# The gate of the S5 branch cut into token chunks, and the first scores' tiles in a pool of their own

## The chip, the cores and the metric

One core of one Trainium2 chip runs the whole step. The metric is device time in microseconds, here the median of three runs; a profile of one execution, with its own time, stands beside it. The core's engines have one instruction stream each: PE (matmuls), ACT (activations), DVE (vector), POOL (a second, slower vector engine), and SP, which here only issues DMA transfers. Each stream is worked off in order, so an instruction that waits holds up all that stand behind it on its engine.

## The reference

One layer over T = 1056 tokens (1024 of a prompt, 32 of a decode step): RMSNorm, one input projection, two branches (attention with 8 heads of 64, and an S5 state-space model), an output projection, a final norm. The part that the change touches is the S5 branch behind its scan:

```
y = gelu(y)
y = y * sigmoid(y @ w_glu + b_glu)                 # the gated linear unit
ssm_o = rmsnorm(y, g_ssm) * silu(gs)               # gs: a slice of the input projection
```

The first attention scores follow in time. They are `z = q @ k.T / 8`, and the weights are built from `sigmoid(z)` and a running product of `sigmoid(-z)` along the keys ("stick breaking", no softmax).

## The kernel before

Tokens are worked in three chunks, `TC = [(0, 256), (256, 384), (640, 416)]`. Channels lie on the 128 partitions, four groups `m` of them, so the S5 output is `y_nat` [128, 4, 1056] in the on-chip memory.

The kernel's order of work is fixed when the program is built. Projections (`proj`) are generators that emit matmuls; beside them run tasks, which are resumed after each step of a projection. A task yields a name (it goes on when that piece of work has been emitted), a number of steps, or a time of a clock kept by rough costs (`at`, `dve`). That clock decides only where in the streams an instruction is put. `put` issues a store one step later on SP's queue.

The stretch in question begins when the scan's last output is in (`open_glu`). Then PE interleaves the matmuls of the gated linear unit (`glu(0)`, `glu(1)`, `glu(2)`, one per chunk, four groups of twelve matmuls `z<-yh`, `z<-yl` each) with the projections q0, k0 and v0 (`pj<-xh,w_hi` and the like), in three chunks each. Each `glu(i)` splits its chunk into a high and a low half (`yh` by ACT, `yl` by DVE); after each group ACT forms the sigmoid `sg`, DVE multiplies it into `y_nat`, ACT squares, and POOL adds the squares up in `sqS`, from which the norm's sum comes.

`ssm_gate` follows `glu2`. For each of the four channel groups it loads `gs` [128, 1056] from DRAM, DVE multiplies `y_nat` by `gssm` and `gs` (one scalar_tensor_tensor), ACT forms `sgs = sigmoid(gs)`, POOL multiplies that in, and the group is stored to `ssm_d`, where it is read much later. Two `gs` tiles exist, in the place of `yl` and `yh`. At the end `sums` turns the squares into one number per token on PE (nine matmuls by a column of ones), and `rsqrt` makes the inverse root `rsS` by six small operations on POOL, on 9 columns (one per 128 tokens).

Then the pool of `y_nat` and of the other temporaries is closed, and the tiles of the attention are laid out in the memory that comes free: `qB1`, `kB1`, `kL1`, `vS1` first, then the two buffers `cb` for the running products, the mask row `own`, and the `betaS` and `betaL` tiles. POOL clears half of `kL1` and most of `own` on the way. The first unit of the attention (`s1_unit`) emits score matmuls `z<-kA,qA`; ACT writes `sigmoid(-z)` into `cb` and `sigmoid(z)` into `betaL`; DVE scans `cb` (with `own`), and POOL multiplies the result into `betaL`, which PE transposes later. PE has two banks for `z`, so it can run at most two score tiles ahead of ACT. The projections that follow are woven in between as filler.

Of the kernel before, what the change touches and what calls it, by code (L numbers as in the profile page):

```python
# [8 lines left out]
F32 = mybir.dt.float32  # L9
F32R = mybir.dt.float32r  # L10
BF = mybir.dt.bfloat16
I32 = mybir.dt.int32
AF = mybir.ActivationFunctionType
# [12 lines left out]
NB = 134  # L26
NK = 25
RSS = 28
LEAD = 1
WARM = 9  # L30
WL = {1: ((1, slice(0, 1)),), 2: ((0, slice(1, 3)), (1, slice(1, 3))), 4: ((0, slice(3, 8)),), 5: ((1, slice(3, 8)),)}
# [188 lines left out]
def hymba_step(ctx, tc, xT, xn, w_in, ln_g, kcT, vc, w_glu, b_glu, w_out, g_att, g_ssm, final_g,  # L220
# [26 lines left out]
    def act(out, in_, f=AF.Copy, **kw):  # L247
        nc.scalar.activation(out, in_, f, **kw)

    def tt(out, a, b, op, eng=None):  # L250
        (eng or nc.vector).tensor_tensor(out, a, b, op)
# [76 lines left out]
    def rsqrt(out, src, inv_n, t1, t2):  # L328
        g = nc.gpsimd
        ts(t1, src, inv_n, EPS, OP.mult, OP.add, g)  # L330
        tt(out, t1, mhalf[:t1.shape[0]].to_broadcast(list(t1.shape)), OP.pow, g)
        tt(t2, out, out, OP.mult, g)
        tt(t2, t2, t1, OP.mult, g)
        ts(t2, t2, -0.5, 1.5, OP.mult, OP.add, g)
        tt(out, out, t2, OP.mult, g)

    def sums(rs, sq):
        pp = p_tr()
        s_, a_, b_ = rsc, rst[:, 0], rst[:, 1]
        nc.vector.memset(s_, 1.0)  # L340
        for b in range(9):
            n = min(128, T - 128 * b)
            nc.tensor.matmul(pp[:n, b:b + 1], sq[:, 128 * b:128 * b + n], ones,
                             start=True, stop=True)
        nc.vector.tensor_copy(s_[:, 0:8], pp[:, 0:8])
        nc.vector.tensor_copy(s_[0:TS, 8:9], pp[0:TS, 8:9])
        rsqrt(rs, s_, 1.0 / 512, a_, b_)

    s2 = ExitStack()
    ss = s2.enter_context(tc.tile_pool(name="ss", bufs=1))  # L350
# [26 lines left out]
    def x_sq(b):  # L377

        m, _ = blk(b)
        nc.scalar.activation(xq[b][:m], xq[b][:m], AF.Square, accum_out=rst[:m, 1, b:b + 1])  # L380

    xq = {}
    rsc = const.tile([128, 9], F32, name="rsc")
# [194 lines left out]
    def at(*aps, lead=0.0):  # L578

        return lambda: nc.ready(*aps) - lead  # L580
# [74 lines left out]
    def put(dst, src):  # L655

        later.append([PUT, lambda: nc.sync.dma_start(dst, src)])
# [85 lines left out]
    with ExitStack() as s1:  # L743
# [449 lines left out]
        def open_glu():  # L1193
            yield "y3"
            yield "GW"
            nc.sync.dma_start(st_out, fin)
            s2.close()
            open_pair0()
            gl = s1.enter_context(tc.tile_pool(name="gl", bufs=1, side="right"))
            G["p"] = gl  # L1200
            Y1["sq"] = gl.tile([128, T], F32, name="sqS")
            done.add("G")

        def lag(m):
# [12 lines left out]
        def glu_y(i):  # L1217
            t0, n = TC[i]
            gl = G["p"]
            yh = gl.tile([128, 4, NM], F32R, name="yh")  # L1220
            yl = gl.tile([128, 4, NM], F32R, name="yl")
            act(yh[:, :, :n], Y1["y"][:, :, t0:t0 + n])
            tt(yl[:, :, :n], Y1["y"][:, :, t0:t0 + n], yh[:, :, :n], OP.subtract)
            YH[i] = yh, yl

        def glu(i):

            yield "G" if i == 0 else f"glu{i - 1}"
            glu_y(i)
            t0, n = TC[i]  # L1230
            yh, yl = YH[i]
            yield at(yh[:, :, :n], yl[:, :, :n], G["h"], G["l"])
            for m in range(4):
                ps = p_z()
                for k in range(4):
                    for f, (a, b) in enumerate(((G["h"], yh), (G["h"], yl), (G["l"], yh))):
                        nc.tensor.matmul(ps[:, :n], a[:, k, m * 128:(m + 1) * 128], b[:, k, :n],
                                         start=(k == 0 and f == 0), stop=(k == 3 and f == 2))
                sg = G["p"].tile([128, NM], F32, name="sg", bufs=2)
                act(sg[:, :n], ps[:, :n], AF.Sigmoid, bias=bglu[:, m:m + 1])  # L1240
                yv = Y1["y"][:, m, t0:t0 + n]
                tt(yv, yv, sg[:, :n], OP.mult)
                sq = Y1["sq"][:, t0:t0 + n]
                if m == 0:
                    act(sq, yv, AF.Square)
                else:
                    act(sg[:, :n], yv, AF.Square)
                    tt(sq, sq, sg[:, :n], OP.add, nc.gpsimd)
                yield 2
            done.add(f"glu{i}")  # L1250

        tg = {}

        def gate_load(m):
            tg[m] = G["p"].tile([128, T], F32, name="gs", tag=("yl", "yh")[m % 2])
            nc.sync.dma_start(tg[m], gs_d[:, m])

        def ssm_gate():
            yield "glu2"
            gate_load(0)  # L1260
            gate_load(1)
            for m in range(4):
                yield at(tg[m], lead=500.0)
                yv = Y1["y"][:, m]
                nc.vector.scalar_tensor_tensor(yv, yv, gssm[:, m:m + 1], tg[m], OP.mult, OP.mult)
                sg = Y1["p"].tile([128, T], F32, name="sgs", tag="bst", bufs=2)
                act(sg, tg[m], AF.Sigmoid)
                tt(yv, yv, sg, OP.mult, gp)
                put(ssm_d[:, m], yv)
                if m < 2:  # L1270
                    gate_load(m + 2)
                yield dve(yv)
            yield at(Y1["sq"])
            sums(rsS, Y1["sq"])

        at_step(2, 20, spawn, glu_weights())
        at_step(6, 0, spawn, open_glu())
        for i in range(3):
            at_step(6, 0, spawn, glu(i))
        at_step(6, 0, spawn, ssm_gate())  # L1280

        def until(f):
            while f not in done:
# [26 lines left out]
    p1 = ctx.enter_context(tc.tile_pool(name="p1", bufs=1))  # L1310
    Q["sqA"] = p1.tile([128, T], F32, name="sqA")
    s3 = ctx.enter_context(ExitStack())
    at = s3.enter_context(tc.tile_pool(name="at", bufs=1))
    qB[1] = at.tile([128, TP], F32R, name="qB1")
    kB[1] = at.tile([128, TP], F32R, name="kB1")
    kL[1] = at.tile([128, TP], F32R, name="kL1")
    nc.gpsimd.memset(kL[1][0:64].bitcast(F32), 0.0)
    vS[1] = at.tile([128, 8, 128], F32, name="vS1")
    NC_ = 2
    cbuf = [at.tile([128, CW], F32, name=f"cb{i}") for i in range(NC_)]  # L1320

    own = at.tile([128, TP], BF, name="own")
    nc.gpsimd.memset(own[:, 0:TP - 128], 0.0)
    nc.vector.tensor_copy(own[:, TP - 128:TP], ident)
    n_c = [0]
# [14 lines left out]
    def beta(n):  # L1340

        if n <= 512:
            return at.tile([128, 512], F32, name="betaS", bufs=2)
        return at.tile([128, CW - 1], F32, name="betaL", bufs=4)

    def c_tile():
        n_c[0] += 1
# [242 lines left out]
    def pipeline():  # L1590

        units = []
        for p in range(4):
            for h in range(2):
                for j in (3, 0, 2, 1):
                    units.append((p, h, j))
                    if (p, h, j) in DEC:
                        units.append(("dec", DEC.index((p, h, j))))
        live = []

        def tail(u, out):
            if u[0] == "dec":
                yield from decode_s3(u[1], out[0])
            else:
                yield from s3_unit(*u, *out)

        for i, u in enumerate(units + [None, None]):
            out = []
            if u is None:
                first = iter(())  # L1610
                n1 = 0
            elif u[0] == "dec":
                first = decode_s1(u[1], out)
                n1 = 6
            else:
                p, h, j = u
                if (h, j) == (0, 3):
                    yield f"qkv{p}"
                ratio[0] = RATIO[2 * p + h]
                first = s1_unit(p, h, j, out)  # L1620
                n1 = 2 * (1 + j // 2)
            second, n3 = iter(()), 0
            if len(live) == 2 or u is None:
                v = live.pop(0)
                second = tail(*v)
                n3 = 13 if v[0][0] == "dec" else 2 * v[0][2] + 2

            if units[i + 1:i + 2] and units[i + 1] and units[i + 1][0] == "dec":
                for n in range(4):
                    k_load(units[i + 1][1], n)  # L1630
            a = b = 0
            e1 = e3 = False
            yield 0.0
            while not (e1 and e3):
                if not e1 and (e3 or a * n3 <= b * n1):
                    a += 1
                    x = next(first, None)
                    e1 = x is None
                else:
                    b += 1  # L1640
                    x = next(second, None)
                    e3 = x is None
                if x is not None:
                    yield x
            if u is not None:
                live.append((u, out))
                if u[0] != "dec" and u[1:] == (0, 1):
                    flags.add(f"A{u[0]}")
                if u[0] != "dec" and u[1:] == (1, 1):
                    flags.add(f"S1_{u[0]}")  # L1650
        while pvq:
            yield pop_pv()
# [415 lines left out]
```

## Time and profile before

| | us |
|---|---|
| median of 3 runs (lowest to highest) | 681.17 (680.73 to 681.33) |
| the profiled execution | 682.8 |
| its span, first to last instruction | 680.9 |
| PE busy in the span | 626.7 (92%) |
| DVE, ACT, POOL busy | 429.1, 346.3, 228.1 |
| mean granted TensorE clock | 0.968 of full |

The profiled execution took 1.9 us more than its span, and 1.6 us more than the median of the runs. PE is the busiest engine by far, so what counts is where it stands still, or runs at the lower of its two clock levels. The page's line of PE and its line of the granted clock show those places, in 40 slices of 17 us each.

### The profile page before, as it was taken

What the parts mean: (1) busy time and instruction counts of PE and PEld (TensorE: products, weight loads), DVE (VectorE), ACT (ScalarE), POOL (GpSimd) and SP (SyncE); (2) the same over time, 40 slices, a digit from 0 to 9 for tenths busy, and PEclk for the clock granted to TensorE, in tenths of its full rate; (3) what the DMA queues carried; (4) which work ended last, traced back from release to release, by engine and by line L of the source; (5) the groups of instructions that cost most, each with busy time, mean ns of one, the idle gap of its engine ahead of it and who ended that gap; (6) DMA issues with size and microseconds to landing.
All of it is one profiled execution on the core that took longest, in us unless ns stands there. A gap on an engine that the chain in (4) does not pass through costs nothing.

```text
span 680.9 us, 10474 instructions
## 1 busy us (share of the span) xinstructions
PE 626.7 (92%) x3760; PEld 523.9 (77%) x3760; DVE 429.1 (63%) x670; ACT 346.3 (51%) x787; POOL 228.1 (33%) x334
## 2 busy tenths in 40 slices
PE   7948999999969993899999999999998899997995
PEld 6938899988969993788878698886775566756873
DVE  5947999889335443465776565656557948364654
ACT  5572423252555643566766657555765645442332
POOL 0011122000122167444345343432417513133885
PEclk7969999999979996999999999999999999998999
DMA  8726342552520144210221112333162795218552
GB/s 307 270 90 175 95 143 79 178 167 66 177 69 24 56 166 153 67 36 25 64 87 59 46 44 74 95 103 102 39 184 92 254 286 178 69 63 269 182 172 100
DMA packets 64132, 83.46 MB, mean 123 GB/s; under 512 B 9040, under 2 KB 47248, under 8 KB 64080
## 3 DMA queue, kind: packets, MB, share of 16 engines
q1 hardware_dynamic: 57600, 71.23, 32.4%
q10 hardware_dynamic: 6480, 11.56, 5.4%
q8 instruction: 30, 0.49, 0.3%
q14 instruction: 22, 0.18, 0.1%
HBM read 56.29 MB, written 26.48 MB: 122 GB/s over the span
## 4 chain that ended last, share of the span: by engine, by line
PE 69%; POOL 6%; DMA 5%; ACT 4%; issue 3%; DVE 3%; SPq 1%; DVEq 0%; POOLq 0%; ACTq 0%
PE pj L215 36%; PE z L215 14%; PE pv L215 10%; PE tr L215 8%; POOL rst L215 2%; DMA gs<-gs_d 1%; DMA x<-in_xn 1%; POOL rsA L215 1%; DMA w_raw<-in_w_in 1%; DMA yj<-yd 1%; DVE cb L215 1%; DMA yd<-Y 1%; SPq L215 1%; POOL s__6538 L215 0%; DMA O<-att_d 0%
## 5 line engine op out<-in xcount | busy, mean ns | idle before, releaser
L215 PE MATMUL pj<-xh,w_hi 128*128 128x256 f32 (+2 forms) x472 | 163.9, 350 | 0.0
L215 PE MATMUL pj<-xl,w_hi 128*128 128x256 f32 (+2 forms) x472 | 151.4, 324 | 0.0
L215 PE MATMUL pj<-xh,w_lo 128*128 128x256 f32 (+2 forms) x472 | 151.3, 323 | 0.0
L215 PEld LDWEIGHTS pj<-xh,w_hi 128*128 128x128 f32 x472 | 89.9, 190 | 23.7 <-issue 19.8
L215 DVE TENSOR_TENSOR_SCAN cb<-cb,own 128x896 f32<-128x896 f32 (+3 forms) x64 | 96.5, 1514 | 15.0 <-ACT cb L215 12.8
L215 PEld LDWEIGHTS pj<-xl,w_hi 128*128 128x128 f32 x472 | 90.2, 191 | 1.7
L215 PEld LDWEIGHTS pj<-xh,w_lo 128*128 128x128 f32 x472 | 89.5, 190 | 0.3
L215 ACT ACTIVATE cb<-z 128x512 f32<-128x512 f32 (+4 forms) x102 | 49.8, 488 | 53.0 <-PE z L215 34.7
L215 PE MATMUL pj<-xh,S 128*128 128x512 f32 (+3 forms) x212 | 69.4, 405 | 2.1 <-DVE x L215 1.5
L215 POOL TENSOR_TENSOR betaL<-betaL,cb 128x896 f32<-128x896 f32 (+2 forms) x24 | 41.4, 1725 | 60.8 <-DVE cb L215 36.9
L215 POOL TENSOR_TENSOR w_lo<-w_raw,w_hi 128x512 fp32r<-128x512 f32 x30 | 46.5, 1550 | 44.3 <-ACT w_hi L215 44.3
L215 ACT ACTIVATE wt<-tr 128x512 f32<-128x512 f32 (+2 forms) x86 | 47.2, 552 | 16.6 <-PE tr L215 16.3
L215 PE MATMUL pv<-wt,vS 128*64 128x256 f32 x320 | 52.0, 404 | 1.1 <-POOL wt L215 1.1
L215 POOL TENSOR_TENSOR betaS<-betaS,cb 128x128 f32<-128x128 f32 (+3 forms) x32 | 27.1, 851 | 73.2 <-DVE cb L215 38.3
L215 PEld LDWEIGHTS pj<-xh,S 128*128 128x128 f32 (+2 forms) x212 | 36.2, 184 | 17.2 <-issue 7.5
L215 DVE TENSOR_TENSOR kv_out<-pj,rsx 128x256 f32<-128x256 f32 (+2 forms) x55 | 28.3, 514 | 29.5 <-PE pj L215 29.0
L215 PE MATMUL pj<-xl,S 128*128 128x512 f32 (+3 forms) x112 | 43.1, 387 | 0.0
L215 ACT ACTIVATE w_hi<-w_raw 128x512 fp32r<-128x512 f32 x44 | 27.6, 630 | 27.0 <-DMA w_raw<-in_w_in 17.0
L215 PE MATMUL tr<-ident,betaL 128*128 128x128 f32 x226 | 35.8, 276 | 4.1 <-ACT wt L215 2.6
L215 ACT ACTIVATE betaL<-z 128x512 f32<-128x512 f32 (+4 forms) x70 | 35.8, 512 | 0.0
L215 PEld LDWEIGHTS tr<-ident,betaL 128*128 128x128 f32 x226 | 26.9, 141 | 11.1 <-ACT wt L215 3.4
L215 DVE TENSOR_TENSOR attT<-pv,attT 64x256 f32<-64x256 f32 x32 | 13.4, 420 | 32.6 <-ACT attT L215 32.4
(273 smaller groups left out, 1273.3 us busy)
## 6 DMA issues: line engine op xcount, KB each, us to landing
w_raw<-in_w_in ACTq DMA_DIRECT2D x44, 256.0 KB, 2.6
xq<-in_xn SPq DMA_DIRECT2D x8, 512.0 KB, 7.4
x<-in_xn SPq DMA_DIRECT2D x8, 512.0 KB, 5.7
yp_d<-x SPq DMA_DIRECT2D x8, 512.0 KB, 2.9
x<-yp_d SPq DMA_DIRECT2D x8, 512.0 KB, 5.2
y_out<-x SPq DMA_DIRECT2D x8, 512.0 KB, 2.9
xr<-in_xT SPq DMA_DIRECT2D x7, 528.0 KB, 8.6
wraw<-in_w_out SPq DMA_DIRECT2D x5, 512.0 KB, 5.3
```

Of the source, the lines that this page charges most:

```text
L215: return g(*args, **kw)
```

## The change

The gate is done chunk by chunk. `gate(i)` is a task that starts when `glu(i)` and `gate(i - 1)` have been emitted, and `glu(2)` now also waits for `gate(0)`. A gate loads its chunk of `gs` in two halves of two channel groups each, into two tiles of their own; per half there are one sigmoid (ACT), two scalar_tensor_tensor (DVE), one product over both groups and one store. The products of chunks 0 and 1 are POOL's, those of chunk 2 DVE's (`GPG`). The squares' tile is per chunk, and `sums` is called per chunk: chunk 0 has 2 columns, chunk 1 has 3, chunk 2 has 4. The root follows at once for chunks 0 and 1. For chunk 2 only the sums are copied out; its root, and the clearing of `kL1`, are issued behind the attention's second unit. The tiles `cb`, `own` and `beta` come from a pool `az`, opened ahead of the pool with `qB1`, `kB1`, `kL1` and `vS1`.

```
+GPG = (1, 1, 0)
-    def sums(rs, sq):
+    def sums(i, rs, sq):
...
+        if i < 2:
+            rsqrt(rs[:, c], s_, 1.0 / 512, a_, b_)
...
+            if i == 2:
+                yield "gate0"
             glu_y(i)
...
+            Y1["sq", i] = G["p"].tile([128, NM], F32, name="sqS", bufs=2)
...
-        def ssm_gate():
-            yield "glu2"
-            gate_load(0)
-            gate_load(1)
-            for m in range(4):
-                yield at(tg[m], lead=500.0)
-                yv = Y1["y"][:, m]
-                nc.vector.scalar_tensor_tensor(yv, yv, gssm[:, m:m + 1], tg[m], OP.mult, OP.mult)
-                sg = Y1["p"].tile([128, T], F32, name="sgs", tag="bst", bufs=2)
-                act(sg, tg[m], AF.Sigmoid)
-                tt(yv, yv, sg, OP.mult, gp)
-                put(ssm_d[:, m], yv)
-                if m < 2:
-                    gate_load(m + 2)
+        def gate(i):
+
+            yield f"glu{i}"
+            if i:
+                yield f"gate{i - 1}"
+            t0, n = TC[i]
+            cs = slice(t0, t0 + n)
+            g = [G["p"].tile([128, 2, NM], F32, name="gs", bufs=2) for _ in range(2)]
+            for h in range(2):
+                nc.sync.dma_start(g[h][:, :, :n], gs_d[:, 2 * h:2 * h + 2, cs])
+            for h in range(2):
+                gh = g[h][:, :, :n]
+                yield at(gh, lead=300.0)
+                sg = Y1["p"].tile([128, 2, NM], F32, name="sgs", tag="bst", bufs=2)
+                act(sg[:, :, :n], gh, AF.Sigmoid)
+                for m in (2 * h, 2 * h + 1):
+                    yv = Y1["y"][:, m, cs]
+                    nc.vector.scalar_tensor_tensor(yv, yv, gssm[:, m:m + 1], gh[:, m % 2], OP.mult, OP.mult)
+                yv = Y1["y"][:, 2 * h:2 * h + 2, cs]
+                tt(yv, yv, sg[:, :, :n], OP.mult, GPG[i] and gp)
+                put(ssm_d[:, 2 * h:2 * h + 2, cs], yv)
                 yield dve(yv)
-            yield at(Y1["sq"])
-            sums(rsS, Y1["sq"])
+            sums(i, rsS, Y1["sq", i])
+            done.add(f"gate{i}")
...
+    az = s3.enter_context(tc.tile_pool(name="az", bufs=1))
+    cbuf = [az.tile([128, CW], F32, name=f"cb{i}") for i in range(2)]
+    own = az.tile([128, TP], BF, name="own")
     at = s3.enter_context(tc.tile_pool(name="at", bufs=1))
...
-    nc.gpsimd.memset(kL[1][0:64].bitcast(F32), 0.0)
...
+            if i == 1:
+                nc.gpsimd.memset(kL[1][0:64].bitcast(F32), 0.0)
+                rsqrt(rsS[:, 5:9], rsc[:, 5:9], 1.0 / 512, rst[:, 0, 5:9], rst[:, 1, 5:9])
```

The order of SP's queue between the last store of `tga_d` and the end of the gate, before (`gs` the gate's loads, `ssm_d` its stores, `kT_out` and `vT_out` the stores of k0 and v0 as their chunks come out):

```order
L215 DMA kT_out<-kv_out_2263 128x416
L215 DMA gs_2350<-gs_d_91 128x1056
L215 DMA gs_2352<-gs_d_91 128x1056
L215 DMA vT_out<-kv_out_2360 128x256
L215 DMA gs_2394<-gs_d_91 128x1056
L215 DMA ssm_d_89<-y_nat_623 128x1056
L215 DMA vT_out<-kv_out_2403 128x384
L215 DMA gs_2436<-gs_d_91 128x1056
L215 DMA ssm_d_89<-y_nat_623 128x1056
L215 DMA vT_out<-kv_out_2445 128x416
```

And of the changed kernel, from the store of k0's second chunk on:

```order
L216 DMA kT_out<-kv_out_2223 128x384
L216 DMA gs_2260<-gs_d_91 128x2x384
L216 DMA gs_2261<-gs_d_91 128x2x384
L216 DMA kT_out<-kv_out_2278 128x416
L216 DMA ssm_d_89<-y_nat_623 128x2x384
L216 DMA vT_out<-kv_out_2340 128x256
L216 DMA vT_out<-kv_out_2430 128x384
L216 DMA ssm_d_89<-y_nat_623 128x2x384
L216 DMA gs_2482<-gs_d_91 128x2x416
L216 DMA gs_2483<-gs_d_91 128x2x416
L216 DMA vT_out<-kv_out_2486 128x416
L216 DMA ssm_d_89<-y_nat_623 128x2x416 x2
```

The loads of chunks 0 and 1 have moved ahead of the rest; the two of the last chunk stand directly behind the second store of chunk 1.

DVE's order from the last products of the linear unit to the first scan of the attention, before (`sg` the linear unit's sigmoid, `kv_out` a projection's chunk taken out of its bank; the row with `cb` and `own` is the scan):

```order
L215 TENSOR_TENSOR y_nat_623<-y_nat_623,sg_2335 128x416
L215 TENSOR_TENSOR kv_out_2360<-pj_2290,rsx_106 128x256
L215 SCALAR_TENSOR_TENSOR y_nat_623<-y_nat_623,gssm_82,gs_2350 128x1056
L215 TENSOR_TENSOR kv_out_2403<-pj_2362,rsx_106 128x384
L215 SCALAR_TENSOR_TENSOR y_nat_623<-y_nat_623,gssm_82,gs_2352 128x1056
L215 TENSOR_TENSOR kv_out_2445<-pj_2405,rsx_106 128x416
L215 SCALAR_TENSOR_TENSOR y_nat_623<-y_nat_623,gssm_82,gs_2394 128x1056
L215 SCALAR_TENSOR_TENSOR y_nat_623<-y_nat_623,gssm_82,gs_2436 128x1056
L215 MEMSET rsc_110 128x9
L215 COPY rsc_110<-tr_2455 128x8
L215 CAST own_2503<-ident_74 128x128
L215 SCALAR_TENSOR_TENSOR cb1_2502<-cb1_2502,own_2503 128x896
```

And of the changed kernel:

```order
L216 TENSOR_TENSOR y_nat_623<-y_nat_623,sg_2419 128x416
L216 TENSOR_TENSOR kv_out_2430<-pj_2342,rsx_106 128x384
L216 SCALAR_TENSOR_TENSOR y_nat_623<-y_nat_623,gssm_82,gs_2261 128x384 x2
L216 COPY rsc_110<-tr_2471 128x3
L216 TENSOR_TENSOR kv_out_2486<-pj_2432,rsx_106 128x416
L216 SCALAR_TENSOR_TENSOR y_nat_623<-y_nat_623,gssm_82,gs_2482 128x416 x2
L216 TENSOR_TENSOR y_nat_623<-y_nat_623,sgs_2488 128x2x416
L216 SCALAR_TENSOR_TENSOR y_nat_623<-y_nat_623,gssm_82,gs_2483 128x416 x2
L216 TENSOR_TENSOR y_nat_623<-y_nat_623,sgs_2493 128x2x416
L216 MEMSET rsc_110 128x4
L216 CAST own_2530<-ident_74 128x128
L216 SCALAR_TENSOR_TENSOR cb1_2529<-cb1_2529,own_2530 128x896
```

The last product of the linear unit now comes when v0's first chunk has long been taken out, and the last chunk's gate products stand on DVE, between its scalings.

On PE the four groups of `glu(2)` begin, before, three matmuls ahead of the end of k0's last chunk, with 3 matmuls of 416 columns and 12 of 256 between the groups; in the changed kernel they begin behind the whole first chunk of v0 (24 matmuls of 256 columns), with 18 of 384 columns of v0's second chunk between the groups. From the first scores on, PE's order is the same in both.

The first `cb` tile's write on ACT waited, before, for the POOL product of the gate and for the stores `ssm_d` of all four groups. In the changed kernel it waits for the last scaling by `gs` on DVE (`gs_2483`), for ACT's sigmoid of the same tile, and for its own scores.

## Rows read from the trace of the kernel before

**Rows 1.** The page's 40 slices: PE's busy share and granted clock, in tenths.
```profile
PE   7948999999969993899999999999998899997995
PEclk7969999999979996999999999999999999998999
```
**Rows 2.** PE in time: start, length, what, idle before and its releaser.
```profile
268.33 0.80 PE L215 MATMUL z<-kA,qA 128*128 128x512 f32 x1 [10.37 <-ACT betaL L215]
...
278.62 0.55 PE L215 MATMUL tr<-ident,betaL 128*128 128x128 f32 x3 [1.45 <-POOL betaL L215]
...
613.68 0.34 PE L215 MATMUL pj<-xh,S 128*64 128x256 f32 x1 [1.46 <-DVE x L215]
...
619.43 0.53 PE L215 MATMUL z<-xh,S 128*128 128x512 f32 x1 [3.17 <-ACT S L215]
```
**Rows 3.** Chain of waits in order of time, 213 to 290 us: start, length, what.
```profile
220.98 1.05 PE pj L215 x6
...
238.84 0.72 PE pj L215 x6
239.56 2.29 PE z L215 x12
...
243.20 4.50 DMA w_raw<-in_w_in
...
261.85 2.41 POOL y_nat L215
...
264.29 2.73 DMA ssm_d<-y_nat
...
267.19 0.60 ACT cb L215
267.79 0.50 ACT betaL L215
```
**Rows 4.** Who waited for whom, 190 to 300 us: total, times, longest.
```profile
PE z L215 <- DVE yl L215: 0.7, 1, 0.7
```
**Rows 5.** POOL in time, 240 to 290 us: columns as in rows 2.
```profile
243.89 1.08 POOL L215 TENSOR_TENSOR sqS<-sqS,sg 128x416 f32<-128x416 f32 x1 [1.48 <-ACT sg L215]
...
250.63 4.86 POOL L215 TENSOR_TENSOR y_nat<-y_nat,sgs 128x1056 f32<-128x1056 f32 x2
...
283.35 1.32 POOL L215 TENSOR_TENSOR betaL<-betaL,cb 128x640 f32<-128x640 f32 x1 [1.60 <-DVE cb L215]
```
**Rows 6.** DVE in time, 240 to 290 us: columns as in rows 2.
```profile
248.21 1.31 DVE L215 SCALAR_TENSOR_TENSOR y_nat<-y_nat,gssm,gs 128x1056 f32<-128x1056 f32 x1
...
253.29 3.31 DVE L215 SCALAR_TENSOR_TENSOR y_nat<-y_nat,gssm,gs 128x1056 f32<-128x1056 f32 x1
...
269.42 2.02 DVE L215 TENSOR_TENSOR_SCAN cb<-cb,own 128x896 f32<-128x896 f32 x1 [1.96 <-POOL own L215]
```
**Rows 7.** The tile `gs`: its four loads on SP (ns), issue to landing.
```profile
L215 SPq DMA_DIRECT2D gs<-gs_d x4: 320/349/722, 241.8 to 254.0; - x4
...
DMA to landing us min/median/max: 3.6/4.3/6.3
```
**Rows 8.** Groups by form: busy us, mean ns of one, idle before.
```profile
L215 DVE TENSOR_TENSOR yl<-y_nat,yh 128x1024 fp32r<-128x1024 f32 x1 | 1.2, 1225 | 4.9 <-ACT yh L215 4.9
...
L215 POOL TENSOR_TENSOR rsA<-rst,mhalf 128x1 f32<-128x1 f32 x8 | 4.4, 555 | 0.7
...
L215 POOL MEMSET kL<- 64x1024 f32 x2 | 1.9, 946 | 0.1
...
L215 POOL TENSOR_TENSOR rsS<-rst,mhalf 128x9 f32<-128x9 f32 x1 | 1.8, 1841 | 0.1
```
**Rows 9.** Stages of 1 us: busy time (count) of five engines, PEclk, DMA.
```profile
271.00:272.00 1.00, 1.00 (x5) 0.95 (x4) 0.77 (x3) 0.00 (x0) 1.00 (x1) 0.70 0.00 0
...
621.00:622.00 1.00, 1.00 (x3) 0.75 (x3) 0.90 (x2) 0.53 (x1) 0.00 (x0) 0.50 0.94 307
```
**Rows 10.** ACT in time, 240 to 290 us: columns as in rows 2.
```profile
289.58 0.49 ACT L215 ACTIVATE cb<-z 128x384 f32<-128x384 f32 x1 [0.40 <-PE z L215]
```

More of the change, by code (lines that the diff above doesn't have):

```diff
@@ L335, in rsqrt @@
         tt(out, out, t2, OP.mult, g)
-    def sums(rs, sq):
+    def sums(i, rs, sq):
         pp = p_tr()
[L339 to L347, printed above, removed]
+        t0, n = TC[i]
+        bs = range(t0 // 128, (t0 + n + 127) // 128)
+        c = slice(bs[0], bs[-1] + 1)
+        s_, a_, b_ = rsc[:, c], rst[:, 0, c], rst[:, 1, c]
+        if i == 2:
+            nc.vector.memset(s_, 1.0)
+        for b in bs:
+            m, e = blk(b)
+            nc.tensor.matmul(pp[:m, b:b + 1], sq[:, e.start - t0:e.stop - t0], ones, start=True, stop=True)
+        nc.vector.tensor_copy(rsc[:, bs[0]:min(8, bs[-1] + 1)], pp[:, bs[0]:min(8, bs[-1] + 1)])
+        if i == 2:
+            nc.vector.tensor_copy(rsc[0:TS, 8:9], pp[0:TS, 8:9])
+        if i < 2:
+            rsqrt(rs[:, c], s_, 1.0 / 512, a_, b_)
     s2 = ExitStack()
@@ L379, in x_sq @@
         m, _ = blk(b)
-        nc.scalar.activation(xq[b][:m], xq[b][:m], AF.Square, accum_out=rst[:m, 1, b:b + 1])
+        s_ = rst[:m, 1, b:b + 1]
+        nc.scalar.activation(xq[b][:m], xq[b][:m], AF.Square, accum_out=s_)
     xq = {}
@@ L1200, in open_glu @@
             G["p"] = gl
-            Y1["sq"] = gl.tile([128, T], F32, name="sqS")
             done.add("G")
@@ L1228, in glu @@
             yield "G" if i == 0 else f"glu{i - 1}"
+            if i == 2:
+                yield "gate0"
             glu_y(i)
@@ L1242, in glu @@
                 tt(yv, yv, sg[:, :n], OP.mult)
-                sq = Y1["sq"][:, t0:t0 + n]
+                sq = Y1["sq", i][:, :n]
                 if m == 0:
@@ L1250, in glu @@
             done.add(f"glu{i}")
[L1252 to L1256, printed above, removed]
-        def ssm_gate():
-            yield "glu2"
-            gate_load(0)
-            gate_load(1)
-            for m in range(4):
-                yield at(tg[m], lead=500.0)
-                yv = Y1["y"][:, m]
-                nc.vector.scalar_tensor_tensor(yv, yv, gssm[:, m:m + 1], tg[m], OP.mult, OP.mult)
-                sg = Y1["p"].tile([128, T], F32, name="sgs", tag="bst", bufs=2)
-                act(sg, tg[m], AF.Sigmoid)
-                tt(yv, yv, sg, OP.mult, gp)
-                put(ssm_d[:, m], yv)
-                if m < 2:
-                    gate_load(m + 2)
+        def gate(i):
+            yield f"glu{i}"
+            if i:
+                yield f"gate{i - 1}"
+            t0, n = TC[i]
+            cs = slice(t0, t0 + n)
[13 more added lines that the diff above has]
+                put(ssm_d[:, 2 * h:2 * h + 2, cs], yv)
                 yield dve(yv)
-            yield at(Y1["sq"])
-            sums(rsS, Y1["sq"])
+            sums(i, rsS, Y1["sq", i])
+            done.add(f"gate{i}")
         at_step(2, 20, spawn, glu_weights())
@@ L1279, in hymba_step @@
             at_step(6, 0, spawn, glu(i))
-        at_step(6, 0, spawn, ssm_gate())
+        for i in range(3):
+            at_step(6, 0, spawn, gate(i))
         def until(f):
@@ L1316, in hymba_step @@
     kL[1] = at.tile([128, TP], F32R, name="kL1")
-    nc.gpsimd.memset(kL[1][0:64].bitcast(F32), 0.0)
     vS[1] = at.tile([128, 8, 128], F32, name="vS1")
     NC_ = 2
-    cbuf = [at.tile([128, CW], F32, name=f"cb{i}") for i in range(NC_)]
-    own = at.tile([128, TP], BF, name="own")
     nc.gpsimd.memset(own[:, 0:TP - 128], 0.0)
@@ L1342, in beta @@
         if n <= 512:
-            return at.tile([128, 512], F32, name="betaS", bufs=2)
-        return at.tile([128, CW - 1], F32, name="betaL", bufs=4)
+            return az.tile([128, 512], F32, name="betaS", bufs=2)
+        return az.tile([128, CW - 1], F32, name="betaL", bufs=4)
     def c_tile():
```

## The prediction

> **What bounds the kernel now.** I read the page first. PE is busy 92% of the span, and in its 40 slices of 17 us it is near full almost everywhere; the deepest dip after the start is the slice from 255 us, with 3 tenths busy at a granted clock of 6 tenths [rows 1]. So a microsecond in which PE is made to work there should be a microsecond of the whole, as long as PE stays the bound behind it. Next I read PE in time: it stands still for 10.37 us, from 257.96 to 268.33, ahead of the first scores `z<-kA,qA`, and for 1.45 us more at 278.62, ahead of the first transposes [rows 2]. The releaser named for the first is ACT's `betaL`, because both banks are full of scores that ACT hasn't read; why ACT doesn't read them stands in the chain of waits. Read backwards from ACT's `cb` at 267.19: the store `ssm_d<-y_nat` of 2.73 us, ahead of it POOL's product into `y_nat` from 261.85 [rows 3], and ahead of that the last `gs` load; these loads took 3.6 to 6.3 us each [rows 7]. The first `cb` lies in memory that `y_nat` and the gate's other tiles still hold, so the end of the gate, its stores included, ends PE's wait.
>
> **Part 1: the linear unit comes later.** Its last twelve matmuls end at 241.85 now [rows 3]. In the changed order twelve more matmuls of 256 columns and eighteen of 384 stand ahead of them: 12 x 0.12 (0.72 for six) + 18 x 0.175 (1.05 for six) = 4.6 us [rows 3]. PE only does other work first. I add 0.4, about half of the 0.7 for which PE once waited for a low half `yl` [rows 4], since the last chunk's halves are now asked for later: +5.0. Should the halves not be ready, PE waits up to 0.7; should they be ready, nothing. I take 0 for the end and keep 0.7 for the range. POOL's last `sqS` then ends not at 244.97 (243.89 + 1.08 [rows 5]) but at 249.95.
>
> **Part 2: the last loads of `gs`.** Behind that `sqS` stands POOL's product for chunk 1's second half, 768 wide instead of 1056: 2.41 [rows 3] x 768/1056 = 1.75. Its scaling on DVE runs beside the `sqS`. Such a scaling took 1.31 us at 248.21, and 3.31 at 253.29, beside two POOL products that ran from 250.63 to 255.49 [rows 5, 6]. So the two scalings may end up to one `sqS` (1.08) late; between 0 and 1.1 I take 0.5, since they start about when the `sqS` does. The product ends at 252.2. SP issues its store, and only then the last two loads of `gs`, which wait in line behind it though their tiles are free; at 0.35 an issue [rows 7] they go out at 252.6 and 253.0. With the middle landing of 4.3 [rows 7] they are in at 256.9 and 257.4. The bounds are the shortest and the longest landing, 3.6 and 6.3; the loads are smaller than before (832 elements a partition instead of 1056), but other loads and stores stand beside them, so I keep the middle one.
>
> The Trainium skill (SBUF — State Buffer, Who interferes with whom) says that a DVE instruction with two inputs from SBUF and a GpSimd instruction that reads SBUF shut each other out for the whole instruction, whichever came first. The trace agrees: 255.49 + 1.31 = 256.80, and the long scaling ended at 256.60 [rows 5, 6]. By that rule chunk 1's scaling would lose all of the 1.08 instead of 0.5, and the forecast below would be 0.6 longer, 674.2.
>
> **Part 3: the last chunk's gate on DVE.** Per half there are two scalings of 416 (1.31 x 416/1056 = 0.52, with the start of an instruction 0.55 each [rows 6]); between them stands the product of 832 on DVE, 1.225 x 832/1024 = 1.0 [rows 8]. From the first landing: 1.1 + 1.0 + 1.1 = 3.2, so 256.9 + 3.2 = 260.1. The sigmoid on ACT takes about as long as two scalings and runs beside them. The last product, its store and the sums follow, but nothing of the scores waits for them now.
>
> **Part 4: a pool of their own.** The first `cb` no longer waits for POOL's product and the store (2.41 and 2.73 in the chain [rows 3]), but for the last scaling. It can be written at 260.1 instead of 267.19: -7.1. PE resumes 1.14 later (268.33 - 267.19 [rows 2, 3]), at 261.2; what PE does before is the same amount of work, so it stands still from 257.96, 3.3 us instead of 10.4. What is late next is still the gate, through `gs`.
>
> **Part 5: the first scan.** It begins at 269.42, 2.23 behind the first `cb`, released by POOL's clearing of `own` [rows 6]. That stood behind the last root and the clearing of `kL`, which are moved away. The scan then needs its second `cb` only: 0.60 + 0.50 + 0.60 = 1.7 [rows 3]. That is -0.5, and it counts, since PE waits another 1.45 for what the scan starts [rows 2].
>
> **Part 6: kL and the root, moved.** The clearing of `kL` takes 0.95. The root's power takes 0.56 on one column and 1.84 on nine [rows 8]; on four I estimate 1.0 from these. With five small operations it is some 3.2 us, put on POOL ahead of the product into `betaL` at 283.35, before which POOL had been idle for 1.60 [rows 5]. The product comes up to 1.6 later; its buffer `cb` is written again at 289.58 [rows 10], where ACT had waited for PE. I take 0, and 1.0 if that cover is gone. The roots of chunks 0 and 1 and their `gs` loads lie in time in which PE has projections to run: 0.
>
> **Part 7: the clock.** After the long wait PE ran at the lower level (1.2 GHz, granted 0.50) until about 271.6; the stage from 271 has 0.70 [rows 9]. From 268.33 that is 3.3 us at half speed, a loss of 1.65. Does a wait of 3.3 us bring the same fall? After the wait of 3.17 at 619.43 the stage from 621 shows 0.50 [rows 2, 9]. One wait is little evidence, but it is the nearest row: I take 0, and keep a gain of 1.65 as the other end.
>
> **The sum.** -7.1 - 0.5 = -7.6. Against the profiled execution's 682.8 (span 680.9 and 1.9 around it) that is 675.2; that execution lies 1.6 above the median, which goes down by the same amount: 681.17 - 7.6 = 673.6.
>
> **The rivals.**
> R1, the clock doesn't fall. If 3.3 us of standing still leave the granted clock at 1.0, 1.65 more is gained: -9.25, 671.9. For it: the wait is a third of the old, and PE works densely until 257.96. Against it: the stretch after 619.43. A wait of 1.46 at 613.68 [rows 2] is too short to speak to it.
>
> R2, the last loads land late. At the longest landing, 6.3 [rows 7], two us are added, and with the full `sqS` in the way 0.6: 673.6 + 2.6 = 676.2. For it: both of the last loads now go out together, within 0.4 us and right behind a store. Against it: they are smaller.
>
> R3, slower. A load of `w_raw` stands in the chain with 4.50 us at 243.20 [rows 3]. In the changed order ACT's high half of such a weight and POOL's low half stand between the linear unit's last groups, so a late weight holds the sigmoids, the `sqS`, the store, and by SP's line the last loads. From 7.6 us of delay on nothing is gained; two such loads in a row, both uncovered, are 9.0: 681.2 + 1.4 = 682.6. Against it: they are issued well ahead, and now more of PE's work lies between them.
>
> R4, the change doesn't do what it says. If the new pool's memory is still held by something that ends where the old did, PE waits as long: 681.2. Against it: the first write of `cb` waits by its semaphores for the last scaling, its sigmoid and its scores alone.
>
> **How the numbers follow.** Forecast 0.47, R1 0.24, R2 0.19, R3 0.05, R4 0.05. The likeliest gives 673.6. Low end: landing 0.7 sooner, no port wait (0.5), and the clock's 1.65 make -10.45, 670.7. High end: landing 2.0 later, port 0.6, POOL 1.0, halves 0.7 make -3.3, 677.9. The range takes in forecast, R1 and R2, 0.90 of the chance. A measurement of this kernel can tell about 0.2%, 1.4 us, from no change. Faster by more: 0.47 + 0.24 + 0.19 = 0.90; within it: R4, 0.05; slower: R3, 0.05; 682.6 lies just beyond that bound.
>
> **What would show it.** Right: PE's wait ahead of the first `z<-kA,qA` is 2 to 5 us; the last twelve `z<-yh`, `z<-yl` end near 247; the chain ahead of the first `cb` goes through a `gs` load issued near 253 and DVE's scaling, not through `ssm_d`; the scan starts 1.7 behind `cb`. Wrong: the wait is at 8 or more (R4, or R3 if `w_raw` stands in the chain); the last loads need over 6 us (R2); the stages behind the restart show a granted 1.00 (R1); or the scores come as early as forecast but a new wait on PE behind 278, for `betaL` 640 or a transpose, gives the time back.

## The result, and the profile after

The changed kernel took 675.25 us (median of 4 runs, 674.09 to 676.30) beside 681.25 us for the kernel before (4 runs, 680.73 to 682.43): a ratio of 0.9909, with a 95% interval of 0.9888 to 0.9930. Run again later beside other runs of before, it took 674.44 against 682.01, 0.9894 (0.9868 to 0.9919). By these ratios that is 6.2 to 7.2 us less. Forecast were 7.6 less, 673.6, in a range of 670.7 to 677.9. The direction, the place and the size hold; the gain came out 0.4 to 1.4 us smaller.

The profiled execution took 674.09 us, its span 672.2. The page's two lines of PE, as in [rows 1]:

```profile
PE   7949999999969997999999999999998899997995
PEclk8969999999979997999999999999999999998999
```

The dip of 3 tenths in the slice from 255 us is now a 7; the slice behind it and one near the start read 9 instead of 8, and the rest is as before. PE in time there (start, length, what, idle before and its releaser), as in [rows 2]:

```profile
255.56 0.28 PE L216 MATMUL pj<-xh,w_lo 128*128 128x256 f32 x1
259.94 0.79 PE L216 MATMUL z<-kA,qA 128*128 128x512 f32 x1 [4.10 <-ACT betaL L216]
...
269.83 0.60 PE L216 MATMUL tr<-ident,betaL 128*128 128x128 f32 x4
```

PE stands still for 4.10 us instead of 10.37, and no longer in front of the transposes (1.45 before). The first line ends at 255.84, where the kernel before still had 2.1 us to go. That is not the change's doing: on every engine the two orders are the same up to the first instruction of the gate (its first load is issued at 191.5), yet PE was ahead of the execution of before long in front of that. Its 401st matmul began at 80.7 instead of 83.0, and the first matmul of the linear unit 2.2 us sooner:

```profile
194.78 0.58 PE L215 MATMUL z<-yh,wgh 128*128 128x256 f32 x1 [5.02 <-ACT yh L215]
```

```profile
192.58 0.58 PE L216 MATMUL z<-yh,wgh 128*128 128x256 f32 x1 [5.14 <-ACT yh L216]
```

In pool_alone and pool_and_kl below, whose orders are also the same up to there, it began at 193.1 and at 198.8; single executions differ that much. So from here on times are counted from that matmul. The next lines are the gate's last steps in the profile after, engine by engine. POOL:

```profile
246.94 1.21 POOL L216 TENSOR_TENSOR sqS<-sqS,sg 128x416 f32<-128x416 f32 x1 [1.25 <-ACT sg L216]
248.72 1.84 POOL L216 TENSOR_TENSOR y_nat<-y_nat,sgs 128x768 f32<-128x768 f32 x1 [0.56 <-DVE y_nat L216]
...
261.24 2.28 POOL L216 TENSOR_TENSOR w_lo<-w_raw,w_hi 128x512 fp32r<-128x512 f32 x1 [1.51 <-ACT w_hi L216]
263.48 1.77 POOL L216 TENSOR_TENSOR betaL<-betaL,cb 128x896 f32<-128x896 f32 x1
267.54 2.00 POOL L216 TENSOR_TENSOR betaL<-betaL,cb 128x1024 f32<-128x1024 f32 x1 [2.29 <-DVE cb L216]
```

SP's queue, and the landing of the six `gs` loads, as in [rows 7]:

```profile
250.59 0.38 SPq L216 DMA_DIRECT2D ssm_d<-y_nat  x1
251.06 1.04 SPq L216 DMA_DIRECT2D gs<-gs_d  x2
```

```profile
DMA to landing us min/median/max: 3.2/4.0/4.7
```

DVE, as in [rows 6], and ACT:

```profile
246.60 1.97 DVE L216 SCALAR_TENSOR_TENSOR y_nat<-y_nat,gssm,gs 128x384 f32<-128x384 f32 x2
...
255.22 1.21 DVE L216 SCALAR_TENSOR_TENSOR y_nat<-y_nat,gssm,gs 128x416 f32<-128x416 f32 x2 [3.11 <-DMA gs<-gs_d]
256.53 1.03 DVE L216 TENSOR_TENSOR y_nat<-y_nat,sgs 128x832 f32<-128x832 f32 x1
257.47 1.21 DVE L216 SCALAR_TENSOR_TENSOR y_nat<-y_nat,gssm,gs 128x416 f32<-128x416 f32 x2
...
260.42 2.03 DVE L216 TENSOR_TENSOR_SCAN cb<-cb,own 128x896 f32<-128x896 f32 x1
...
264.92 2.83 DVE L216 TENSOR_TENSOR_SCAN cb<-cb,own 128x1024 f32<-128x1024 f32 x2 [2.01 <-ACT cb L216]
```

```profile
258.80 0.60 ACT L216 ACTIVATE cb<-z 128x512 f32<-128x512 f32 x1 [1.02 <-DVE y_nat L216]
```

The chain reads as it was forecast: last `sqS`, POOL's product, the store, the two loads, DVE's scalings, the first `cb`; and the store of the last chunk is no longer in it. The granted clock, stage by stage (columns as in [rows 9]):

```profile
258.00:259.00 1.00, 0.00 (x0) 0.00 (x0) 0.90 (x3) 0.20 (x1) 0.12 (x1) 1.00 0.52 193
259.00:260.00 1.00, 0.06 (x1) 0.07 (x1) 0.89 (x3) 1.00 (x3) 0.73 (x1) 0.63 0.64 233
...
265.00:266.00 1.00, 1.00 (x5) 1.00 (x5) 1.00 (x1) 0.37 (x1) 0.25 (x1) 0.50 0.56 147
266.00:267.00 1.00, 1.00 (x8) 1.00 (x7) 1.00 (x1) 0.45 (x2) 0.00 (x0) 0.95 0.30 115
```

With 0.63 in the stage from 259 and 0.95 in the one from 266, it fell at about 259.3, ahead of PE's restart, and rose at 266.1. From its restart at 259.94 PE ran at the lower level (1.2 GHz) for 6.2 us, a loss of 3.1, where before it lost 1.65 [rows 9]. That looks like 1.4 us given back. The experiments show that hardly any of it is.

### The profile page after: what moved, and what is told of

Read it like the earlier page. It is cut to its first block, busy times and chain, and to the rows that moved or that the text cites. A ratio compares the mean times of both kernels' runs of the same rounds, so it can differ in the third digit from the quotient of the medians.

```text
span 672.2 us, 10493 instructions
## 1 busy us (share of the span) xinstructions
PE 627.3 (93%) x3760; PEld 524.2 (78%) x3760; DVE 431.3 (64%) x682; ACT 346.5 (52%) x789; POOL 226.5 (34%) x346
```

## The experiments

One stretch tells most of it (not all, as the last two kernels show): from the first matmul of the linear unit to the end of POOL's second product into `betaL` (128x1024), for which PE's transposes wait. Before it ends at 276.56 + 2.00 = 278.56:

```profile
276.56 2.00 POOL L215 TENSOR_TENSOR betaL<-betaL,cb 128x1024 f32<-128x1024 f32 x1 [2.29 <-DVE cb L215]
```

Of every profile (one execution each) and of the timed runs, us:

| kernel | first `z<-yh` to first `cb` | first `cb` to second product's end | sum | ratio to before (95%) |
|---|---|---|---|---|
| before | 72.4 | 11.4 | 83.8 | 1 |
| changed | 66.2 | 10.7 | 77.0 | 0.9909 (0.9888 to 0.9930) |
| changed_again | 66.9 | 10.7 | 77.6 | 0.9894 (0.9868 to 0.9919) |
| pool_alone | 67.1 | 16.8 | 83.9 | 1.0030 (0.9995 to 1.0065) |
| pool_and_kl | 67.4 | 12.4 | 79.8 | 0.9932 (0.9902 to 0.9961) |
| no_pool | 70.2 | 10.7 | 80.9 | 0.9948 (0.9925 to 0.9971) |
| kl_root_back | 66.1 | 15.0 | 81.1 | 0.9969 (0.9945 to 0.9993) |
| clock_fill | 67.0 | 10.8 | 77.8 | 0.9922 (0.9895 to 0.9948) |
| products_pool | 66.7 | 12.0 | 78.7 | 0.9938 (0.9912 to 0.9964) |
| pool_delay | 66.4 | 11.9 | 78.3 | 0.9917 (0.9886 to 0.9948) |
| gs_ahead | 61.9 | 11.0 | 72.9 | 0.9842 (0.9791 to 0.9892) |
| gs_ahead_again | 62.1 | 11.0 | 73.1 | 0.9850 (0.9810 to 0.9891) |
| gs_ahead_dve | 63.4 | 11.6 | 75.0 | 0.9830 (0.9798 to 0.9862) |
| gs_ahead_pool | 60.5 | 14.3 | 74.8 | 0.9908 (0.9872 to 0.9944) |

**The parts one by one.** pool_alone is the kernel before with the new pool and nothing else:

```
+    az = s3.enter_context(tc.tile_pool(name="az", bufs=1))
+    cbuf = [az.tile(...) ...]; own = az.tile(...)      # betaS, betaL from az too
```

> The kernel before, with only the tiles cb, own, betaS and betaL in a pool of their own. Theory A (the pool frees the scores, but the first scan still waits for own, which POOL clears behind its last product, the root and kL): the first cb comes some 5.4 us earlier (when the last scaling by gs is done, not the last store), PE's wait ahead of the first scores falls from 10.4 to about 5, the first scan stays at about 269.4, and PE then waits some 3 us or more ahead of the first transposes instead of 1.45. Gain about 2.3 us: 679.0. Theory B (the first scores' wait is all that counts, so the pool is most of the change): gain 5 us or more, 676 or less.

```profile
261.26 0.79 PE L215 MATMUL z<-kA,qA 128*128 128x512 f32 x1 [4.86 <-ACT betaL L215]
271.19 0.44 PE L215 MATMUL tr<-ident,kv_out 128*128 128x128 f32 x2 [2.43 <-DVE cb L215]
273.20 0.50 PE L215 MATMUL z<-kA,qA 128*128 128x512 f32 x1 [1.04 <-ACT betaS L215]
```

```profile
267.72 3.10 DVE L215 TENSOR_TENSOR_SCAN cb<-cb,own 128x896 f32<-128x896 f32 x1 [5.07 <-POOL own L215]
```

PE's wait fell from 10.4 to 4.9, as in theory A, and nothing was gained (1.0030), less than either theory forecast. The first scan waited 5.07 us for `own`, behind POOL's product, root and `kL`; PE met that at 271.19 and 273.20. A wait that is taken away at the first scores only moves to the next step of the same line.

no_pool is the changed kernel with these tiles back in the one pool:

```
+    cbuf = [at.tile(...) ...]; own = at.tile(...)      # behind vS1; betaS, betaL from at too
```

> The changed kernel with cb, own, betaS and betaL back in the one pool behind qB1, kB1, kL1 and vS1. Theory A (the pool and the chunked gate each carry part): the first cb waits again for the stores of y_nat, about 4 us later than in the changed kernel; PE's wait is about 8 us; time about 679.3, between the two kernels. Theory B (the chunked gate alone does it): 675.3 as the changed kernel, PE's wait about 4 us.

```profile
262.91 0.60 ACT L216 ACTIVATE cb<-z 128x512 f32<-128x512 f32 x1 [4.85 <-DMA ssm_d<-y_nat]
```

Theory A: the first `cb` waits for the store, 4 us later from the start of the linear unit (70.2 against 66.2). Measured 678.99, expected 679.3; 0.9948 leaves 3.5 us of the gain of 6.2 to 7.2.

kl_root_back is the changed kernel with

```
+    nc.gpsimd.memset(kL[1][0:64].bitcast(F32), 0.0)     # at the tile, as before
...
-        if i < 2:
+        if True:
             rsqrt(rs[:, c], s_, 1.0 / 512, a_, b_)
...
-            if i == 1:
-                nc.gpsimd.memset(kL[1][0:64].bitcast(F32), 0.0)
-                rsqrt(rsS[:, 5:9], ...)
```

> The changed kernel with the clearing of kL1 and the root of the last chunk at their old place, ahead of own on POOL. Theory A (they stand on the path through own and the first scan): the clearing waits for the last stores of y_nat and the first scan starts some 4 us later, at about 264.5; the wait ahead of the first scores stays 4.1; PE waits about 4 us ahead of the first transposes; time about 679. Theory B (PE has enough other work ahead of the transposes): 675.3, no change against the changed kernel.

```profile
259.08 0.80 PE L216 MATMUL z<-kA,qA 128*128 128x512 f32 x1 [4.14 <-ACT betaL L216]
...
272.97 0.55 PE L216 MATMUL tr<-ident,betaL 128*128 128x128 f32 x3 [1.91 <-POOL betaL L216]
```

```profile
263.68 3.10 DVE L216 TENSOR_TENSOR_SCAN cb<-cb,own 128x896 f32<-128x896 f32 x1 [4.24 <-POOL own L216]
```

```profile
261.92 0.94 POOL L216 MEMSET kL<- 64x1024 f32 x1
262.81 0.84 POOL L216 MEMSET own<- 128x896 bf16 x1
```

Theory A again: PE's first wait is the same 4.1, but the scan stands 5.7 us behind the first `cb` (257.94) instead of 1.6, and 0.6% of the 0.9% gain is gone. One step of the theory was wrong: `kL` did not wait for the stores of `y_nat`. POOL cleared it at once behind the root, which could start only at 259.39, when DVE had copied out the sums, and took 2.4 us. Beside the chunked gate and the pool, moving the clearing and the root was worth about 4 us, not the 0.5 that the prediction gave it.

pool_and_kl is the kernel before with the pool, and with clearing and root (taken out at their old places) behind the second unit; the gate stays by channel groups:

```
             if i == 1:
+                nc.gpsimd.memset(kL[1][0:64].bitcast(F32), 0.0)
+                rsqrt(rsS, rsc, 1.0 / 512, rst[:, 0], rst[:, 1])
```

> The kernel before with the tiles in their own pool and with the clearing of kL1 and the whole root (9 columns) behind the second unit; the gate as before, by channel groups. Theory A (these two take what the pool alone lost: own then stands behind POOL's last product only): the first cb about 5.4 us earlier than before, the first scan at about 3.4 us behind it (own behind the product) instead of 2.2, the transposes about 4.4 us earlier; 677, 0.9935 of before. Theory B (without the chunks nothing is gained, as with the pool alone): 1.000.

Measured: 678.62, 0.9932; expected 0.9935. The first scan began 3.4 us behind the first `cb`, as expected:

```profile
266.15 0.57 ACT L215 ACTIVATE cb<-z 128x512 f32<-128x512 f32 x1
```

```profile
269.55 2.90 DVE L215 TENSOR_TENSOR_SCAN cb<-cb,own 128x896 f32<-128x896 f32 x1
```

So the pool, which does nothing alone, makes some 4.6 of the 6.2 to 7.2 us together with the moved POOL work. (The moved work alone was not run.) The gate by chunks adds the rest, some 2 us by the ratios and 2.2 to 2.8 by the stretch in the table; since the intervals of the ratios overlap, the timed runs alone don't show this last part.

**The clock.** clock_fill puts sixteen matmuls that nobody reads into PE's wait; changed_again is the changed kernel beside it.

```
+        if nz[0] == 3:                     # third tile of scores
+            pp = p_tr()
+            for _ in range(16):
+                nc.tensor.matmul(pp[:, :512], mms[0][0], mms[0][1], start=True, stop=True)
```

> The changed kernel once more, unaltered, as the measure for the others of this call. All theories: 0.991 of the kernel before (about 675); PE's wait ahead of the third tile of scores about 4 us, and a stretch of some 6 us at the lower clock level that begins about when PE resumes.

> The changed kernel with sixteen matmuls more (128x512, a score of the first unit computed again into a bank that nobody reads) ahead of the third tile of scores, where PE waits 4.1 us. They take about 16 x 0.22 = 3.5 us, so they fit into the wait. Theory A (the clock falls because PE stands still, and costs 3 us behind the wait): the granted clock stays 1.00, what PE does behind the wait takes 3 us less; gain 3 us against the changed kernel (0.986 of the kernel before); perhaps 0.5 less where the transposes' products then come too late for PE. Theory B (the clock falls for another reason than PE's standing still, or the time comes back as a wait ahead of the transposes): as the changed kernel or up to 0.5 us slower.

PE of clock_fill, and its stage from 262 us:

```profile
259.68 3.94 PE L217 MATMUL tr<-kA,qA 128*128 128x512 f32 x16 [2.26 <-ACT kv_out L217]
...
271.46 0.55 PE L217 MATMUL tr<-ident,betaL 128*128 128x128 f32 x3 [0.72 <-POOL betaL L217]
```

```profile
262.00:263.00 1.00, 1.00 (x6) 0.82 (x5) 0.88 (x4) 1.00 (x3) 0.00 (x0) 1.00 0.42 158
```

The clock stayed at 1.00 and nothing was gained (0.9922 against 0.9894, intervals that overlap). The filling began 2.26 us late, released by ACT's `kv_out`, which was read from the bank's earlier content, and ended at 263.62. So PE also restarted late: the third tile of scores began 2.8 us behind the first `cb` (263.47 against 260.65) instead of 1.1, which could hide a gain. The trace shows that it did not: PE was still early by the 0.72 us that it waited for the second product, and that product ended 10.8 us behind the first `cb`, as in the changed kernel. changed_again says the same from the other side: there the lower level began 0.2 us ahead of PE's restart at 260.76 and lasted until 264.0, 3.4 us in all and not 6.8:

```profile
260.00:261.00 1.00, 0.24 (x1) 0.24 (x2) 0.89 (x5) 1.00 (x4) 0.55 (x1) 0.79 0.44 160
...
263.00:264.00 1.00, 1.00 (x5) 1.00 (x4) 0.69 (x3) 0.10 (x1) 1.00 (x1) 0.51 0.00 0
264.00:265.00 1.00, 1.00 (x7) 0.91 (x6) 0.00 (x0) 0.33 (x1) 1.00 (x2) 1.00 0.34 123
```

```profile
270.40 0.55 PE L216 MATMUL tr<-ident,betaL 128*128 128x128 f32 x3 [0.81 <-POOL betaL L216]
```

and PE, faster there, waited 0.81 for the product instead. With a loss of 3.1 us, of 1.6, or of none, the stretch from `cb` to the product is 10.7 to 10.8. Theory B holds, in its second form: what is lost or saved in clock there comes back as a wait in front of the transposes. These began 11.0 us behind the first `cb` with the loss of 3.1 (269.83), and 10.8 with the others (270.40 here, 271.46 in clock_fill), so the clock cost a few tenths of a us at most.

Why the line doesn't feel PE's speed stands in its middle. The second scan needs a tile of scores from PE, and this did come 0.4 us sooner with the shorter loss. But POOL's first product into `betaL` was then still running:

```profile
264.30 1.77 POOL L216 TENSOR_TENSOR betaL<-betaL,cb 128x896 f32<-128x896 f32 x1
```

```profile
265.30 3.26 DVE L216 TENSOR_TENSOR_SCAN cb<-cb,own 128x1024 f32<-128x1024 f32 x2 [1.57 <-ACT cb L216]
```

The scan began 0.8 us ahead of that product's end (266.07), in the changed kernel 0.3 ahead of it (264.92 against 265.25), and ended no sooner for it: the two lines, which hold this scan and the short next one, end 8.9 us behind the first `cb` in either (268.56 and 267.75). In both kernels, and in clock_fill, the second product starts 2.3 us behind the end of the first, and 2.29 is what this scan takes with POOL's product out of its way (pool_delay, below).

**The line behind the first `cb`.** products_pool gives the last chunk's products to POOL (`GPG = (1, 1, 1)`).

> The changed kernel with the last chunk's two products on POOL instead of DVE. The first cb waits for the last scaling alone, which then has one product of 1.0 us less in front of it: the first cb and PE's restart about 1 us sooner. Theory A (own stands behind both products on POOL, about 1.9 us each, and the scan behind own): own is cleared about 2 us later than now, the first scan starts 1.5 to 2 us later and PE waits ahead of the transposes; time 675 to 677. Theory B (only the first cb counts): 1 us faster, 674.

```profile
255.19 4.05 DVE L216 SCALAR_TENSOR_TENSOR y_nat<-y_nat,gssm,gs 128x416 f32<-128x416 f32 x4 [3.05 <-DMA gs<-gs_d]
```

```profile
256.55 2.25 POOL L216 TENSOR_TENSOR y_nat<-y_nat,sgs 128x832 f32<-128x832 f32 x1 [2.59 <-DVE y_nat L216]
259.38 1.95 POOL L216 TENSOR_TENSOR y_nat<-y_nat,sgs 128x832 f32<-128x832 f32 x1 [0.59 <-DVE rsc L216]
261.26 0.85 POOL L216 MEMSET own<- 128x896 bf16 x1
```

677.16, just above theory A's range; the first `cb` was not 1 us sooner, and the scan began 3.0 behind it instead of 1.6. The four scalings took 4.05 us instead of 2.4, since the second pair ran into POOL's product: that ended at 258.80, and the scalings at 259.24.

pool_delay clears `kL1` three times ahead of the first product into `betaL`:

```
+        for _ in range(3):                 # in the first s1_fin only
+            nc.gpsimd.memset(kL[1][0:64].bitcast(F32), 0.0)
         tt(be[:, :n], be[:, :n], c[:, o + 1:CW], OP.mult, nc.gpsimd if n in GPW else None)
```

> The changed kernel with kL1 cleared three times (0.95 us each, 2.85 in all) on POOL directly ahead of the attention's first product into betaL, instead of once behind the second unit. Theory A (from the first cb on, the line through the scans and POOL's products sets PE's transposes, and PE's own work, at half clock or not, fits beside it): the first transposes of betaL come 2.5 to 2.85 us later, PE waits that long there, time 0.990 x before + 2.6 us (about 0.994). Theory B (PE's restart and its clock set it, the line has room): no change, 0.990.

```profile
264.14 2.95 POOL L216 MEMSET kL<- 64x1024 f32 x3
267.06 4.35 POOL L216 TENSOR_TENSOR betaL<-betaL,cb 128x896 f32<-128x896 f32 x2
```

By the profile both theories missed: of 2.95 us only 1.2 arrived (11.9 against 10.7). The time, 0.9917, can't be told from the changed kernel's, nor from theory A's 0.994. In the changed kernel the second scan runs behind the first product, and POOL stands idle for 2.29 us ahead of the second. Here the scan, begun at 265.60, took its 2.29 us for the most part while POOL cleared, and both products followed it, so most of the delay fell into POOL's idle time. The line is the bound, but with a rest of some 1.7 us in it that shows only when its order changes.

**A faster version.** gs_ahead issues each chunk's loads as soon as the tile's last reader is emitted, ahead of the store:

```
...
+                if i < 2:
+                    gate_load(i + 1, h)        # dma_start into the next chunk's tile
                 put(ssm_d[:, 2 * h:2 * h + 2, cs], yv)
```

> The changed kernel with each chunk's load of gs issued as soon as the tile's last reader of the chunk before is emitted, ahead of that chunk's store, so that the last two loads don't stand behind the store that waits for POOL's product. Theory A (the loads set the end of the gate, and the clock falls because of the wait of 4.1 us): the first cb is free by about 254 to 255, PE's wait goes to 0 to 1 us, the granted clock stays 1.00 in the stages after it, which gives back 3 us more; time about 668. Theory B (the wait goes but the clock falls nonetheless): 671. Theory C (scalings that now run beside the linear unit and POOL's sums delay these): wait still 2 us or more, 673 to 675.

> The kernel with the last gs loads ahead once more, unaltered, as the measure for the next one and for a tighter interval. All theories: 0.983 to 0.986 of the kernel before; no stage at the lower clock level around the first scores; PE's waits there 1.1 and 1.8 us.

```profile
253.22 0.66 PE L216 MATMUL tr<-ident,kv_out 128*128 128x128 f32 x4 [1.06 <-DVE kv_out L216]
264.09 0.50 PE L216 MATMUL z<-kA,qA 128*128 128x512 f32 x1 [1.78 <-ACT betaS L216]
```

```profile
254.52 0.60 ACT L216 ACTIVATE cb<-z 128x512 f32<-128x512 f32 x1
```

671.91 (0.9842) and 671.35 (0.9850): some 3 to 4.5 us below the changed kernel by medians and ratios (the intervals overlap a little). PE's wait ahead of the third tile is gone and the granted clock stayed at 1.00, but the time is theory B's 671 and not A's 668. B's reason was wrong, though (the clock did not fall); by the experiments above it is rather that the clock wasn't the bound, which was not tested here. Two attempts on top of it, `GPG = (1, 1, 1)` as in products_pool, and

```
-        tt(be[:, :n], be[:, :n], c[:, o + 1:CW], OP.mult, nc.gpsimd if n in GPW else None)
+        tt(be[:, :n], ..., nc.gpsimd if n in GPW and not_first else None)
```

> The last loads of gs issued ahead, and the last chunk's products on POOL. With the loads ahead PE waited 1.06 us for a k/v chunk that DVE took out behind the first scalings and a product, and 1.78 later. Theory A (DVE is what is late there): without the products on DVE the first of these waits goes, gain 0.5 to 1 us against the loads ahead alone (0.983 of the kernel before). Theory B (POOL is late: own behind the products): the scan starts 1 us or more later, no gain or a loss of 1 us (0.984 to 0.986).

> The last gs loads ahead, and the attention's first product into betaL (896 columns) on DVE instead of POOL. Theory A (with the gate out of the way, the line first cb, scan on DVE, product on POOL, second scan, second product sets when PE gets its transposes; the first product on POOL and the second scan on DVE shut each other out): the product takes about 1.1 us on DVE behind its scan, the second scan ends about when it does now or 0.2 later, and POOL's second product starts at once instead of behind the first: 1.3 us sooner; PE's wait of 1.78 goes; gain 1.3 us against the loads ahead alone. Theory B (PE is the bound there): no change, or a loss of up to 1 us for DVE's added work.

With the products on POOL, `own` came behind them, the first scan began 5.1 us behind the first `cb`, and by the medians all that the loads ahead had gained was lost (0.9908, with intervals that overlap a little). With the first product on DVE the result, 0.9830, can't be told from 0.9850: the product took 1.94 us, not 1.1, beside POOL's `w_lo`,

```profile
262.67 1.94 DVE L216 TENSOR_TENSOR betaL<-betaL,cb 128x896 f32<-128x896 f32 x1
```

so theory A's gain is not shown. The stretch in the table orders these two wrongly: 74.8 for the slower, 75.0 for the faster, and 72.9 for gs_ahead. It is read from one execution each, and the profiles of these two have 3.4 us at the lower clock level, in or behind the stretch, that gs_ahead's has not.

That `glu(2)` waits for `gate(0)` was not tried alone.

## Why the prediction was right, and where its sizes were off

**Parts 1 and 2, the later linear unit and the loads: right.** With the 2.2 us of shift added, the linear unit's last matmul group ends at 246.9 (forecast 246.85), the last `sqS` at 250.35 (249.95), POOL's product at 252.8 (252.2), the loads go out at 253.3 (252.6) and the first scaling starts at 257.4 (256.9). POOL idled 0.56 for the scaling, where 0.5 was taken between 0 and 1.1. The full exclusion that the Trainium skill states (SBUF — State Buffer, Who interferes with whom) is in the rows nonetheless: the two scalings took 1.97, while two somewhat wider ones took 1.21 beside an idle POOL; the first had begun ahead of the `sqS`, which lost time itself (1.21 instead of 1.08).

**Parts 3 and 4, the first `cb`: right, 0.9 too early.** It came 3.6 behind the first scaling's start (forecast 3.2) and, shifted, at 261.0 instead of 260.1: 0.4 from the later `sqS`, 0.4 from DVE's steps, the rest from product and issue, less 0.1 for faster loads. PE's wait is 4.1 where 3.3 was forecast. That is the term that was mis-sized: -7.1 was -6.2 in this profile and -5.5 in changed_again (72.4 against 66.2 and 66.9 in the table).

**Part 5, the scan: right in size** (1.62 behind the first `cb`, forecast 1.7; the whole line to the product 0.6 to 0.7 shorter, forecast 0.5).

**Part 6: right as a sum, too narrow as an account.** The moved clearing and root cost nothing at their new place. But the working valued their leaving at 0.5, as if `own` had only stood in the way of the scan by that much; with an earlier `cb` they would have held the scan back by about 4 us: it began 5.7 us behind the first `cb` in kl_root_back and 1.6 without them, 7.6 in pool_alone and 3.4 in pool_and_kl. In the sum this is hidden, since the change moves both.

**Part 7: the step was wrong in kind, though its 0 was right.** The clock fell near the end of the wait of 4.1 us, as it had fallen around the 3.17 in [rows 2], but the loss, larger than the old one, cost a few tenths of a us at most. R1 priced a clock that doesn't fall at 1.65 us of gain; clock_fill, where it didn't, shows none. The prediction had the 1.45 us in front of the transposes [rows 2] in view and used it to count the scan's 0.5, but not to see that PE's own speed ahead of it was covered.

R2 to R4 did not occur: the longest `gs` load took 4.7; the sigmoids of the linear unit's last groups waited for PE alone, at most 1.5 us, and not for a weight; and the pool did what it says.

## What to carry to other kernels

Take the wait that a trace shows, then walk the line behind it: what is freed at one step waits at the next for whatever still stands in that engine's queue, so an edit that is worth nothing alone, as the pool was here, can be worth much beside another. Where PE waits at the end of a stretch, nothing that speeds PE up inside the stretch counts, its clock included. And a load queued behind a store that waits for something else is late for no reason of its own: issuing it ahead gave as much again as half of the whole change.

## What was not expected of the hardware

One and the same program had the lower clock level for 6.8 us in one execution and for 3.4 in another, around waits of PE of 4.10 and 4.24 us. gs_ahead_dve showed it too, for 3.4 us from 255.4 on, around a wait of only 1.06 us, while gs_ahead, with the same wait, kept 1.00. Whether the clock falls around a wait, and for how long, could not be read from one neighbouring case, as the prediction tried.
